# Low-rank products of a hybrid decoder: float32r parts at the start of the mixing, results kept in DRAM

## The chip, the cores and the metric

The kernel runs on one core of a Trainium2 chip. Time is in device microseconds of one execution, lower is better. Engines are named as in the profile: PE (TensorE matmul) and PEld (its weight loads), DVE (VectorE), ACT (ScalarE), POOL (GpSimd) and SP, whose queue issues nearly all DMAs.

## The reference, cut to what matters

One step of a one-layer decoder: a half-step SwiGLU FFN, a token mixing with three branches (RWKV-7, a convolution, a cross-attention into 256 memory tokens), and a second FFN. The kernel handles 512 prompt tokens and 64 sample tokens side by side, N = 576 columns, with channels on partitions. In the RWKV branch three low-rank products matter here:

```
wd, ad, gd = xm[..., c3:c4], xm[..., c4:c5], xm[..., c5:]      # 64, 64 and 160 wide
w_log = -jax.nn.softplus(-(p['w0'] + jnp.tanh(wd) @ p['w_decay_up'])) - 0.5
decay = jnp.exp(-jnp.exp(w_log))                               # = exp(-0.6065 * sigmoid(...))
a = jax.nn.sigmoid(p['a0'] + ad @ p['w_a_up'])
g = jax.nn.sigmoid(gd) @ p['w_g_up']
...
y_a = (o.reshape(b, t, D_RWKV) * g) @ p['w_rwkv_out']
```

`xm` is the token-shifted projection of the input; each product has 512 output channels, that is four blocks of 128 (one block is a pair of heads). `decay` and `a` enter the recurrence, `g` multiplies its normalised output.

## The kernel before, in words

The first FFN runs to about 430 us, the mixing from there to about 990, the merge of the branches and the second FFN after it. Large products are made of float32r parts: an operand is split into a high part, rounded to float32r by a cast on ACT (line 96), and a low part, the difference, on DVE (line 97). Three matmuls (high x high, high x low, low x high) into one PSUM bank give the product (line 110); the columns go in two halves of 288 (`H`). `proj` loads a weight block of 8 x 128 columns, splits it in pieces of 512 and makes 2 x 24 such matmuls. Small products take plain float32 operands, through `full` (line 128), which makes one matmul per operand pair and half of the columns.

The mixing starts in `lora`: `shifted(12)`, `shifted(13)` and `shifted(14)` project the low-rank inputs (win 12 holds wd and ad, 13 and 14 hold gd; 14 is only 32 wide), apply the token shift, and leave `la` (tanh on its first half) and `lg` (sigmoid). Then a list of steps, `PLAN`, runs: `A` attention, `P` `prep` of a block, `I` `inverse` and `J` `joined` of a small triangular matrix, `B` `chain` (the recurrence and the output), `G`, `C` the convolution, and `X`, `Y`, `Z`, gate projections that fill PE. In `prep` the sigmoid of `w` (tile sg, buffers u1) comes from `full("g", wda[:64], la[:64])`, then Exp, scan and reciprocal; `av` comes from `full("g", wda[64:], la[64:])`. In `chain` the gate comes last: `full("c", wg0 x lg0, wg1 x lg1)`, and DVE multiplies the result from PSUM into rs. The PSUM tags of the mixing are p (three banks, projections), g (two, prep) and c (three, chain and attention).

The order on each engine is not the order of the text: a scheduler lays the instructions of all steps on the engines by priority and by its own estimates of their durations, and each engine then runs its list strictly in order. Tiles of one name share buffers, so an instruction may also wait for a buffer's last reader. SP's list holds loads and stores alike, and a store that waits for its data holds back the loads behind it.

Of the kernel before, what the change touches and what calls it, by code (L numbers as in the profile page):

```python
# [6 lines left out]
F32 = mybir.dt.float32  # L7
F32R = mybir.dt.float32r
AF = mybir.ActivationFunctionType
ALU = mybir.AluOpType  # L10
# [40 lines left out]
class _Builder:  # L51
# [60 lines left out]
    def proj(self, src, x, n=8, m=128):  # L112

        w = self.wload(src, n * m)
        ps = []
        for h in range(2):
            p = self.bank()[:m, :H]
            self.mm3(p, w, x, n, h, m)
            ps.append((slice(h * H, (h + 1) * H), p))
        return ps  # L120
# [53 lines left out]
    def build(self):  # L174
        tc, a = self.tc, self.a
        with ExitStack() as st:
# [14 lines left out]
            self.d_g0 = [dr.tile([128, N], F32, name=f"d_g0{i}") for i in range(8)]  # L191
            self.d_ya = [dr.tile([128, N], F32, name=f"d_ya{i}") for i in range(4)]

            s_mem = ExitStack()
# [391 lines left out]
    def shifted(self, m, out, zp):  # L586

        V, A = self.V, self.A
        rows = 32 if m == 14 else 128
        p = self.proj(self.a["w14"] if m == 14 else self.a["win"][m], self.xn, 8, rows)  # L590
# [14 lines left out]
    def lora(self, lp):  # L605
        A, a = self.A, self.a
        self.ssh = lp.tile([128, 15, NB], F32, name="ssh")
        self.sho = lp.tile([128, 15, 9], F32, name="sho")
        self.wda = lp.tile([128, 512], F32, name="wda")
        self.wg = [lp.tile([128, 512], F32, name="wg0"), lp.tile([128, 512], F32, name="wg1")[:32]]  # L610
        self.G.memset(self.sho[:, 14, :], 0.0)
        self.dma(self.ssh, a["ssh"])
        self.dma(self.wda, a["wda"])
        self.dma(self.wg[0], a["wg0"])
        self.dma(self.wg[1], a["wg1"])
        self.la = lp.tile([128, N], F32, name="la")
        aux = lp.tile([128, 600], F32, name="aux")
        self.lg = [lp.tile([128, N], F32, name="lg0"), aux[:32, :N]]
        self.t11 = aux[64:96, :N].rearrange("p (h c t) -> p h c t", h=2, c=9)
        self.zz = aux[96:128, :16 * 33].rearrange("p (h c t) -> p h c t", h=2, c=8)  # L620
        self.z = [lp.tile([128, SEQ + 81], F32, name=f"z{i}") for i in range(2)]
        self.gi = lp.tile([128, PADN], F32, name="gi")
        self.st = [lp.tile([128, 128], F32, name=f"st{i}") for i in range(3)]
        self.ms = lp.tile([128, NB, 128], F32, name="ms")
        self.ax = lp.tile([128, 9, 64], F32, name="ax")
        for t in self.z:
            self.G.memset(t[:, 0:1], 0.0)
        self.G.memset(self.gi, 0.0)
        for t in self.padded(self.gi):
            self.G.memset(t[:, :, 0:1], 1.0)  # L630
        for t in self.st + [self.ms, self.ax]:
            self.G.memset(t, 0.0)
        with self.tc.tile_pool(name="lz", bufs=1, side="right") as zp:
            self.shifted(12, self.la, zp)
            A.activation(self.la[:64], self.la[:64], AF.Tanh)
            for i in range(2):
                self.shifted(13 + i, self.lg[i], zp)
                A.activation(self.lg[i], self.lg[i], AF.Sigmoid)

# [172 lines left out]
    def prep(self, j):  # L812
# [12 lines left out]
        sg = b1.tile([128, 640], F32, name="u1", bufs=2)[:, :N]  # L825
        for c, p in self.full("g", (self.wda[:64, 128 * j:128 * j + 128], self.la[:64])):
            A.activation(sg[:, c], p, AF.Sigmoid, bias=par("w0", j))
        w = b1.tile([128, PADN], F32, name="w")
# [10 lines left out]
        av = tmp("av")  # L839
        for c, p in self.full("g", (self.wda[64:, 128 * j:128 * j + 128], self.la[64:])):  # L840
            A.activation(av[:, c], p, AF.Sigmoid, bias=par("a0", j))

# [55 lines left out]
    def chain(self, j):  # L898
# [36 lines left out]
        V.tensor_tensor(rs, rs, bv, ALU.add)  # L935
        ch = slice(128 * j, 128 * j + 128)
        for c, p in self.full("c", (self.wg[0][:, ch], self.lg[0]), (self.wg[1][:, ch], self.lg[1])):
            V.tensor_tensor(rs[:, c], p, rs[:, c], ALU.mult)
        self.dbg(f"ya{j}", rs)
# [193 lines left out]
def _prep(inp):  # L1133
# [32 lines left out]
    for i in "12":  # L1166
# [4 lines left out]
    a["win"] = wt(np.concatenate([win[:, :1792], win[:, 1824:]], axis=1))  # L1171
    a["w14"] = wt(win[:, 1792:1824], 32)[0]
    a["wya"] = wt(f["w_rwkv_out"])
    a["wcb"] = wt(f["w_conv_out"])
    a["woc"] = wt(f["w_xattn_out"])
    a["wo"] = wt(f["w_o"])
    a["wda"] = np.concatenate([f["w_decay_up"], f["w_a_up"]])
    a["wg0"] = np.ascontiguousarray(f["w_g_up"][:128])
    a["wg1"] = np.ascontiguousarray(f["w_g_up"][128:])
    cols = [vec(f["ffn1_norm"]), vec(f["mix_norm"]), vec(f["ffn2_norm"]), vec(f["final_norm"]), vec(f["mu_shift"])]  # L1180
    cols += [vec(f[n].reshape(-1)) for n in ("w0", "a0", "k_k", "k_a", "r_k", "gn_g", "gn_b", "glu_b")]
# [3 lines left out]
    a["ssh"] = np.ascontiguousarray(  # L1185
        np.concatenate([f["state_shift"], np.zeros((NB, 96), f["state_shift"].dtype)], axis=1)
        .reshape(NB, 15, 128).transpose(2, 1, 0))
# [63 lines left out]
```

## Time and profile before

| what | value |
|---|---|
| median of 3 runs | 1480.89 us (1479.6 to 1481.0) |
| the profiled execution, own time | 1484.21 us |
| its span, first to last instruction | 1482.4 us |
| granted clock, mean over the span | 0.985 |
| PE busy | 1464.2 us (99%) |
| DVE, ACT busy | 1026.1 us (69%), 676.2 us (46%) |
| moved by DMA | 144.06 MB, mean 97 GB/s |

The page gives each engine's busy time, the chain of work that ended last, and groups of instructions by source line. A row of a view in order of time begins with the start in us from the span's start and a length; a row of a group has a count (x), then after the bar the busy time in us, the mean of one in ns, and the idle time before it with what ended it. A plain float32 matmul of the program stands as two records in the trace, a float32r one as one. Rows of windows give, for a stretch, the busy us of PE, PEld, DVE, ACT and POOL with counts, then the granted PE clock, the DMA share and GB/s.

### The profile page before, as it was taken

Reading aid. Unit: us, or ns where it says so; the run is one execution under the profiler, and the core shown is the slowest. Engines: PE = TensorE matmul, PEld = TensorE weight load, DVE = VectorE, ACT = ScalarE, POOL = GpSimd, SP = SyncE. Lnnn points to the kernel's source line nnn. Section 1 sums busy time; section 2 is a strip of 40 time slices with the busy share of each in tenths; the row PEclk is TensorE's granted clock in tenths of the full one; section 3 lists DMA queues with packets and bytes.
Section 4 is the critical chain, followed back from the end, with each engine's and each line's share of the span. In section 5 each row is a group of like instructions: output and inputs, shape, how many; then the busy total and the mean of one; then the engine's idle time right before and its main releaser. Section 6 shows DMA issues by size and latency. Waiting matters only on the chain.

```text
span 1482.4 us, 27100 instructions
## 1 busy us (share of the span) xinstructions
PE 1464.2 (99%) x10820; PEld 1382.3 (93%) x10820; DVE 1026.1 (69%) x2054; ACT 676.2 (46%) x1371; POOL 4.7 (0%) x22
## 2 busy tenths in 40 slices
PE   9999999999999999999999999999999999999998
PEld 9999999999998799878889878789999999999997
DVE  7976777777783569769456456357578766777775
ACT  7443434444577535445446533443354433444342
POOL 0000000000010000000000000000000000000000
PEclk9999999999999989999999999999999999999999
DMA  6222222233632244123223124345322322323221
GB/s 210 72 80 92 87 86 86 86 91 102 202 105 86 65 132 83 55 80 105 62 61 109 55 85 137 96 161 189 102 73 72 100 73 85 100 89 98 86 86 65
DMA packets 95179, 144.06 MB, mean 97 GB/s; under 512 B 43645, under 2 KB 53501, under 8 KB 95053
## 3 DMA queue, kind: packets, MB, share of 16 engines
q1 hardware_dynamic: 94476, 141.74, 31.1%
q8 instruction: 85, 1.39, 0.4%
q10 hardware_dynamic: 576, 0.59, 0.1%
q14 instruction: 42, 0.34, 0.1%
HBM read 126.07 MB, written 16.23 MB: 96 GB/s over the span
## 4 chain that ended last, share of the span: by engine, by line
PE 92%; DVE 4%; ACT 1%; DMA 1%; issue 1%; SPq 0%; DVEq 0%; POOL 0%; ACTq 0%; POOLq 0%
PE p L110 51%; PE p L382 26%; PE c L1027 1%; PE g L893 1%; PE c L1031 1%; PE c L1024 1%; DVE pr L986 1%; PE c L128 1%; PE c L1059 1%; PE g L128 1%; PE c L1057 1%; DVE cc L676 1%; PE c L1079 1%; DVE tt L988 1%; PE c L1042 1%
## 5 line engine op out<-in xcount | busy, mean ns | idle before, releaser
L110 PE MATMUL p<-x,wh 128*128 128x288 f32 x3136 | 655.6, 300 | 1.3 <-ACT kv L562 0.7
L110 PEld LDWEIGHTS p<-x,wh 128*128 128x128 f32 x3136 | 507.2, 189 | 15.2 <-issue 7.1
L110 PE MATMUL p<-x,wl 128*128 128x288 f32 x1568 | 470.0, 300 | 1.5 <-DVE wl L97 1.5
L96 ACT CAST wh<-w 128x512 fp32r<-128x512 f32 (+1 forms) x353 | 209.8, 600 | 261.9 <-PE p L382 99.8
L97 DVE TENSOR_TENSOR wl<-w,wh 128x512 fp32r<-128x512 f32 (+1 forms) x353 | 232.4, 663 | 117.4 <-ACT wh L96 110.4
L110 PEld LDWEIGHTS p<-x,wl 128*128 128x128 f32 x1568 | 295.4, 189 | 7.1 <-issue 3.1
L382 PE MATMUL p<-t,wh 128*128 128x288 f32 x1088 | 224.3, 298 | 0.0
L382 PEld LDWEIGHTS p<-t,wh 128*128 128x128 f32 x1088 | 173.8, 188 | 6.4 <-DVE t L393 6.4
L382 PE MATMUL p<-b,wh 128*128 128x288 f32 x816 | 169.7, 295 | 0.0
L382 PE MATMUL p<-t,wl 128*128 128x288 f32 x544 | 160.6, 295 | 0.0
L96 ACT CAST wh<-p 128x512 fp32r<-128x512 f32 x136 | 84.5, 621 | 156.1 <-PE p L110 117.7
L382 PEld LDWEIGHTS p<-b,wh 128*128 128x128 f32 x816 | 132.6, 188 | 0.0
L97 DVE TENSOR_TENSOR wl<-p,wh 128x512 fp32r<-128x512 f32 x136 | 93.7, 689 | 50.1 <-ACT wh L96 47.4
L382 PE MATMUL p<-b,wl 128*128 128x288 f32 x408 | 120.3, 295 | 0.0
L382 PEld LDWEIGHTS p<-t,wl 128*128 128x128 f32 x544 | 102.4, 188 | 0.0
L382 PEld LDWEIGHTS p<-b,wl 128*128 128x128 f32 x408 | 76.8, 188 | 0.0
L460 DVE SCALAR_TENSOR_TENSOR x<-p,x 128x288 f32<-128x288 f32 x128 | 57.9, 453 | 20.0 <-PE p L110 19.9
L96 ACT CAST x<-t 128x576 fp32r<-128x576 f32 (+1 forms) x60 | 36.5, 610 | 45.0 <-DVE t L464 41.8
L1051 DVE SCALAR_TENSOR_TENSOR st<-c,gc,mg 64x64 f32<-64x64 f32 x56 | 15.9, 284 | 53.3 <-PE c L1042 52.5
L372 DVE TENSOR_TENSOR p<-w 128x512 f32<-128x512 f32 x68 | 46.7, 687 | 4.2 <-DMA w<-wu 3.8
L372 DVE TENSOR_TENSOR p<-p,w 128x512 f32<-128x512 f32 x68 | 46.5, 683 | 0.2 <-DMA w<-wu 0.2
L676 DVE SCALAR_TENSOR_TENSOR cc<-up,pv,cc 128x512 f32<-128x512 f32 x60 | 43.9, 750 | 0.1
(354 smaller groups left out, 1990.8 us busy)
## 6 DMA issues: line engine op xcount, KB each, us to landing
w<-wu SPq DMA_DIRECT2D x85, 512.0 KB
w<-win SPq DMA_DIRECT2D x44, 512.0 KB
w<-wd SPq DMA_DIRECT2D x64, 256.0 KB
w<-wd SPq DMA_DIRECT2D x16, 384.0 KB
d_mb<-gate SPq DMA_DIRECT2D x16, 288.0 KB
w<-wo SPq DMA_DIRECT2D x8, 512.0 KB
d_x<-x SPq DMA_DIRECT2D x16, 144.0 KB
d_g<-gate SPq DMA_DIRECT2D x8, 288.0 KB
```

What stands on the lines that cost most here:

```text
L96: self.A.copy(hi, x)
L97: self.V.tensor_tensor(lo, x, hi.bitcast(F32), ALU.subtract)
L110: self.T.matmul(p, l, x[r][:, c], start=k == 0 and i == 0, stop=k == n - 1 and i == 2)
L128: self.T.matmul(p, l, r[:, c], start=i == 0, stop=i == len(ops) - 1)
L372: V.tensor_tensor(s, u, v, ALU.add)
L382: self.T.matmul(p, hl[l][:, c], xs[k][b][:, o], start=first and k == 0 and q == 0, stop=k == 3 and q == 2, skip_group_check=True)
L460: V.scalar_tensor_tensor(x[m][:, c], p, 0.5, x[m][:, c], ALU.mult, ALU.add)
L676: V.scalar_tensor_tensor(c[:, :SEQ], up[:, k:k + SEQ], w, c[:, :SEQ], ALU.mult, ALU.add)
L893: T.matmul(ps[:, i * 128:(i + 1) * 128], kb[o, c + i].rearrange("p a t -> p (a t)"), ra[o, c + i].rearrange("p a t -> p (a t)"), start=Tru ...
L986: V.tensor_tensor(pr, tt[:, :n, :e].unsqueeze(2).broadcast_to([np_, n, m, e]), l3[:, t:e, :e].unsqueeze(1).broadcast_to([np_, n, m, e]), A ...
L988: V.tensor_reduce(tt[:, :n, t:e], pr, op=ALU.add, axis=AX.X)
L1051: V.scalar_tensor_tensor(mn[s, s], ps[s, 256 + 64 * h:320 + 64 * h], gc[s, c:c + 1], mg[s, s], ALU.mult, ALU.add)
```

## The change

All low-rank products are made once, in a new function `low_rank`, right behind the three shifted projections at the start of the mixing. They are made of float32r parts whose low parts are stacked beside high ones: `xs` holds for wd (and for ad) the high part in 64 rows and the low part in the other 64, and the weights `wh` stand twice, so that one 128-row matmul makes high x high plus high x low, and a 64-row one (`wl`) the third term. For the gate, 128 of its 160 inputs take three matmuls, and the other 32, whose projection is now made three times over (96 weight columns), take one matmul of 96 rows. The tanh stays where it was. Sigmoids are applied to w and a as they leave PSUM; the gate is copied. All results go to DRAM: `d_w`, `d_a`, `d_gt`, four blocks each, 288 KB per block. `prep` loads `d_w` and `d_a` in place of its products, with Exp, scan and all that follows as before; `chain` loads `d_gt` and multiplies from SBUF. The tiles `wda`, `wg`, `la`, `lg` are gone from the pool lp; the pool of the new operands, lz, lies where the pool of block 0's tiles lies later, and no longer in the attention's room. Splits of a weight block cut at a multiple of its column width, which alters only the 96-wide one (pieces of 480 and 288).

```diff
     def proj(self, src, x, n=8, m=128):
-        w = self.wload(src, n * m)
+        w = self.wload(src, n * m, 512 // m * m)
...
     def shifted(self, m, out, zp):
-        rows = 32 if m == 14 else 128
+        rows = 96 if m == 14 else 128
...
-        with self.tc.tile_pool(name="lz", bufs=1, side="right") as zp:
-            self.shifted(12, self.la, zp)
-            A.activation(self.la[:64], self.la[:64], AF.Tanh)
-            for i in range(2):
-                self.shifted(13 + i, self.lg[i], zp)
-                A.activation(self.lg[i], self.lg[i], AF.Sigmoid)
+        with self.tc.tile_pool(name="lz", bufs=1) as zp:
+            self.low_rank(zp)
+
+    def low_rank(self, zp):
...
+        x = b1.tile([128, N], F32, name="k")
+        self.shifted(12, x, b1)
+        A.activation(x[:64], x[:64], AF.Tanh)
+        for i in range(2):
+            o, q = slice(64 * i, 64 * i + 64), slice(64 - 64 * i, 128 - 64 * i)
+            A.copy(xs[o, i], x[o])
+            sub(xs[q, i], x[o], xs[o, i])
+        x = b1.tile([128, N], F32, name="r")
+        self.shifted(13, x, b1)
+        A.activation(x, x, AF.Sigmoid)
+        self.split(lg[:, 0], lg[:, 1], x)
+        x = b1.tile([128, N], F32, name="av")[:96]
+        self.shifted(14, x, b1)
+        A.activation(x, x, AF.Sigmoid)
+        A.copy(gs[:96], x)
+        sub(gs[32:64], x[32:64], gs[32:64])
+
+        t = b1.tile([128, 1024], F32, name="lt")
+        self.dma(t, a["wda"])
+        t = t.rearrange("p (i c) -> p i c", i=2)
+        A.copy(wh, t)
+        for i in range(2):
+            o = slice(64 * i, 64 * i + 64)
+            sub(wl[o], t[o, i], wh[o, i])
+        t = [b1.tile([128, PADN], F32, name=n)[:, :512] for n in ("w", "g")]
+        for i in range(2):
+            self.dma(t[i], a["wg"][:, 512 * i:512 * i + 512])
+            A.copy(gh[:, i], t[i])
+        sub(gl, t[0], gh[:, 0])
+        sub(gh[64:96, 1], t[1][64:96], gh[64:96, 1])
+
+        def products(*ops):
+            for h in range(2):
+                c = slice(h * H, (h + 1) * H)
+                p = self.bank("g")[:, :H]
+                for q, (l, r) in enumerate(ops):
+                    T.matmul(p, l, r[:, c], start=q == 0, stop=q == len(ops) - 1)
+                yield c, p
+
+        for j in range(4):
+            ch = slice(128 * j, 128 * j + 128)
+            for i, (par, out, name) in enumerate((("w0", self.d_w, "bv"), ("a0", self.d_a, ("k", "r")[j % 2]))):
+                t = b1.tile([128, N], F32, name=name, bufs=2 - i)
+                o = slice(64 * i, 64 * i + 64)
+                for c, p in products((wh[:, i, ch], xs[:, i]), (wl[o, ch], xs[o, i])):
+                    A.activation(t[:, c], p, AF.Sigmoid, bias=self.par(par, j))
+                self.store(out[j], t)
+            t = b1.tile([128, N], F32, name=("av", "zt")[j % 2])
+            for c, p in products((gh[:, 0, ch], lg[:, 0]), (gh[:, 0, ch], lg[:, 1]), (gl[:, ch], lg[:, 0]),
+                                 (gh[:96, 1, ch], gs[:96])):
+                A.copy(t[:, c], p)
+            self.store(self.d_gt[j], t)
...
     def prep(self, j):
-        for c, p in self.full("g", (self.wda[:64, 128 * j:128 * j + 128], self.la[:64])):
-            A.activation(sg[:, c], p, AF.Sigmoid, bias=par("w0", j))
+        self.dma(sg, self.d_w[j])
...
-        for c, p in self.full("g", (self.wda[64:, 128 * j:128 * j + 128], self.la[64:])):
-            A.activation(av[:, c], p, AF.Sigmoid, bias=par("a0", j))
+        self.dma(av, self.d_a[j])
...
     def chain(self, j):
-        ch = slice(128 * j, 128 * j + 128)
-        for c, p in self.full("c", (self.wg[0][:, ch], self.lg[0]), (self.wg[1][:, ch], self.lg[1])):
-            V.tensor_tensor(rs[:, c], p, rs[:, c], ALU.mult)
+        gt = b3.tile([128, N], F32, name="gt")
+        self.dma(gt, self.d_gt[j])
+        V.tensor_tensor(rs, gt, rs, ALU.mult)
```

Three places show how the change moves instructions. On PE, at the end of the projection of `shifted(14)`, before:

```order
L110 MATMUL p<-x_4958,wh 32x288
L110 MATMUL p<-x_4957,wl 32x288
L110 MATMUL p<-x_4943,wh 128x288
L110 MATMUL p<-x_4944,wh 128x288
L110 MATMUL p<-x_4943,wl 128x288
```

and now (g is the PSUM tag of the products):

```order
L110 MATMUL p<-x_4970,wh 96x288
L110 MATMUL p<-x_4969,wl 96x288
L678 MATMUL g<-xs,wh 128x288
L678 MATMUL g<-xs,wl 128x288
L678 MATMUL g<-xs,wh 128x288
L678 MATMUL g<-xs,wl 128x288
L110 MATMUL p<-x_4955,wh 128x288
L110 MATMUL p<-x_4956,wh 128x288
L110 MATMUL p<-x_4955,wl 128x288
L110 MATMUL p<-x_4957,wh 128x288
L678 MATMUL g<-xs,wh 128x288
L678 MATMUL g<-xs,wl 128x288
```

Where the attention's query projections followed at once, products now stand between and among them; all but the gate products of the last block stand ahead of the first attention score (c<-kT), which follows the same number of projection matmuls as before.

On ACT, behind the token shift of `shifted(12)`: the cast of `wh` from the loaded wda (tile lt), the tanh, the casts of xs, and only then the second piece of the split of the 96-wide weights, where before a cast of 256 stood ahead of that token shift:

```order
L603 ACTIVATE zt<-z_5312,pv 128x584
L597 COPY z_5312<-ssh 96x8
L662 CAST wh<-lt 128x1024
L644 ACT_TABLE_LOAD
L644 ACTIVATE k<-k 64x576
L647 CAST xs<-k 64x576 x2
L598 COPY z_5311<-p 128x288
L599 COPY z_5311<-p 128x224
L600 COPY z_5311<-p 128x8x8
L96 CAST wh<-w 128x288
```

Further on in ACT's list the Exp of `prep` of block 0 (line 886) stands among the sigmoids (687) and gate copies (692) of the products:

```order
L692 COPY av<-g 128x288 x2
L687 ACTIVATE bv<-g,pv 128x288 x2
L687 ACTIVATE r<-g,pv 128x288
L886 ACT_TABLE_LOAD
L886 ACTIVATE w<-u_6204 128x8x64
L687 ACT_TABLE_LOAD
L687 ACTIVATE r<-g,pv 128x288
L692 COPY zt<-g 128x288
```

Its sample columns follow later with a table load before and one behind; before, the two Exp of block 0 stood behind the first softmax, and the sigmoids of a behind them.

On SP, from the load of ssh on, the loads of the weights of the products, and the stores with the first reload (u is the tile that the Exp of block 0 reads; in front of ssh two kc and two vc loads of the attention now stand, which came behind the third of the win loads before):

```order
L820 DMA kc<-ck 128x512 x2
L833 DMA vc<-cv 128x512 x2
L613 DMA ssh<-ssh 128x120
L660 DMA lt<-wda 128x1024
L668 DMA w<-wg 128x512
L668 DMA g<-wg 128x512
L86 DMA w<-win 128x1024
...
L86 DMA w<-win 128x1024 x2
L688 DMA d_w_104<-bv 128x576
L688 DMA d_a_108<-k 128x576
L881 DMA u_6204<-d_w_104 128x576
L693 DMA d_gt_112<-av 128x576
```

The reload of the first block of w stands behind the store of the first block of a; the later reloads stand some places ahead of the loads that their block needs.

More of the change, by code (lines that the diff above doesn't have):

```diff
@@ L192, in build @@
             self.d_ya = [dr.tile([128, N], F32, name=f"d_ya{i}") for i in range(4)]
+            self.d_w = [dr.tile([128, N], F32, name=f"d_w{i}") for i in range(4)]
+            self.d_a = [dr.tile([128, N], F32, name=f"d_a{i}") for i in range(4)]
+            self.d_gt = [dr.tile([128, N], F32, name=f"d_gt{i}") for i in range(4)]
             s_mem = ExitStack()
@@ L605, in lora @@
     def lora(self, lp):
-        A, a = self.A, self.a
+        a = self.a
         self.ssh = lp.tile([128, 15, NB], F32, name="ssh")
         self.sho = lp.tile([128, 15, 9], F32, name="sho")
-        self.wda = lp.tile([128, 512], F32, name="wda")
-        self.wg = [lp.tile([128, 512], F32, name="wg0"), lp.tile([128, 512], F32, name="wg1")[:32]]
         self.G.memset(self.sho[:, 14, :], 0.0)
         self.dma(self.ssh, a["ssh"])
[L613 to L616, printed above, removed]
         aux = lp.tile([128, 600], F32, name="aux")
-        self.lg = [lp.tile([128, N], F32, name="lg0"), aux[:32, :N]]
         self.t11 = aux[64:96, :N].rearrange("p (h c t) -> p h c t", h=2, c=9)
@@ L632, in lora @@
             self.G.memset(t, 0.0)
-        with self.tc.tile_pool(name="lz", bufs=1, side="right") as zp:
-            self.shifted(12, self.la, zp)
-            A.activation(self.la[:64], self.la[:64], AF.Tanh)
-            for i in range(2):
-                self.shifted(13 + i, self.lg[i], zp)
-                A.activation(self.lg[i], self.lg[i], AF.Sigmoid)
+        with self.tc.tile_pool(name="lz", bufs=1) as zp:
+            self.low_rank(zp)
+    def low_rank(self, zp):
+        V, A, T, a, b1 = self.V, self.A, self.T, self.a, self.b1
+        two = lambda name, n: zp.tile([128, 2, n], F32R, name=name)
+        sub = lambda o, x, hi: V.tensor_tensor(o, x, hi.bitcast(F32), ALU.subtract)
+        wh, wl, gh, gl = two("wh", 512), zp.tile([128, 512], F32R, name="wl"), two("gh", 512), zp.tile(
+            [128, 512], F32R, name="gl")
+        xs, lg, gs = two("xs", N), two("lg", N), zp.tile([128, N], F32R, name="gs")
+        x = b1.tile([128, N], F32, name="k")
[47 more added lines that the diff above has]
+            self.store(self.d_gt[j], t)
@@ L1171, in _prep @@
     a["win"] = wt(np.concatenate([win[:, :1792], win[:, 1824:]], axis=1))
-    a["w14"] = wt(win[:, 1792:1824], 32)[0]
+    a["w14"] = wt(np.concatenate([win[:, 1792:1824]] * 3, axis=1), 96)[0]
     a["wya"] = wt(f["w_rwkv_out"])
@@ L1176, in _prep @@
     a["wo"] = wt(f["w_o"])
[L1177 to L1180, printed above, removed]
+    a["wda"] = np.concatenate([np.concatenate([f[n]] * 2) for n in ("w_decay_up", "w_a_up")], axis=1)
+    g = f["w_g_up"]
+    a["wg"] = np.concatenate([g[:128], np.concatenate([g[128:]] * 3 + [np.zeros_like(g[128:])])], axis=1)
+    cols = [vec(f["ffn1_norm"]), vec(f["mix_norm"]), vec(f["ffn2_norm"]), vec(f["final_norm"]), vec(np.concatenate([f["mu_shift"]] + [f["mu_shift"][-32:]] * 2))]
     cols += [vec(f[n].reshape(-1)) for n in ("w0", "a0", "k_k", "k_a", "r_k", "gn_g", "gn_b", "glu_b")]
@@ L1185, in _prep @@
     a["ssh"] = np.ascontiguousarray(
-        np.concatenate([f["state_shift"], np.zeros((NB, 96), f["state_shift"].dtype)], axis=1)
+        np.concatenate([f["state_shift"]] + [f["state_shift"][:, -32:]] * 2 + [np.zeros((NB, 32), np.float32)], axis=1)
         .reshape(NB, 15, 128).transpose(2, 1, 0))
```

## The prediction

> **What bounds the kernel now.** I read the page's shares and clock row first, then the chain of waits, then who waits on PE, and only then single stretches.
>
> ```profile
> span 1482.4 us, 27100 instructions
> PE 1464.2 (99%) x10820; PEld 1382.3 (93%) x10820; DVE 1026.1 (69%) x2054; ACT 676.2 (46%) x1371; POOL 4.7 (0%) x22
> PE 92%; DVE 4%; ACT 1%; DMA 1%; issue 1%; SPq 0%; DVEq 0%; POOL 0%; ACTq 0%; POOLq 0%
> PE c L1008 <- DMA aux<-s: 2.0, 1, 2.0
> PE p L110 <- DVE wl L97: 1.5, 3, 1.1
> PE g L128 <- ACT u L827: 0.5, 2, 0.3
> ```
>
> PE is busy 99% of the span, 92% of the chain is PE, and the longest waits of PE (the last three rows, first number) are 2.0 us and less. Fillers stand between the steps of the recurrence, so a microsecond of PE work taken away anywhere is a microsecond of the span, as long as PE gets no new wait. ACT (46%) and DVE (69%) have room on average; whether they have it where the change puts its work is the question.
>
> **What is removed from PE.** The eight plain float32 products of a block of channels (two for w, two for a, four for the gate; half of the columns each) stand in the trace so, in a view of PE in order of time (start, length, instructions merged):
>
> ```profile
> 455.64 1.23 PE L128 MATMUL g<-la,wda 64*128 64x288 f32 x4
> 456.80 0.40 PE L110 MATMUL p<-x,wh 128*128 128x288 f32 x1
> 457.13 1.23 PE L128 MATMUL g<-la,wda 64*128 64x288 f32 x4
> 458.29 0.40 PE L110 MATMUL p<-x,wh 128*128 128x288 f32 x1
> 458.53 0.29 PE L110 MATMUL p<-x,wl 128*128 128x288 f32 x1
> ...
> 661.08 0.75 PE L128 MATMUL c<-lg,wg 128*128 128x288 f32 x2
> 661.76 0.75 PE L128 MATMUL c<-aux,wg 32*128 32x288 f32 x2
> 662.44 0.75 PE L128 MATMUL c<-lg,wg 128*128 128x288 f32 x2
> 663.12 0.75 PE L128 MATMUL c<-aux,wg 32*128 32x288 f32 x2
> 663.80 0.40 PE L110 MATMUL p<-x,wl 128*128 128x288 f32 x1
> 664.04 0.43 PE L110 MATMUL p<-x,wh 128*128 128x288 f32 x2
> 664.31 0.29 PE L110 MATMUL p<-x,wl 128*128 128x288 f32 x1
> 664.43 0.43 PE L110 MATMUL p<-x,wh 128*128 128x288 f32 x2
> 664.70 0.29 PE L110 MATMUL p<-x,wl 128*128 128x288 f32 x1
> ```
>
> Lengths overlap, so starts must be subtracted. From wl at 664.31 to wl at 664.70 are three float32r matmuls: 0.39/3 = 0.13 us each. A plain float32 product is two records. The w and a products of block 0 take 458.53 - 455.64 = 2.89, less two float32r matmuls that stand among them, 2.89 - 0.26 = 2.63 us; the gate products 664.04 - 661.08 = 2.96, less one, 2.83 us. Four blocks: 4 x (2.63 + 2.83) = 21.8 us. With the 0.5 us that PE waited at L128 for ACT, 22.3 us go.
>
> **What is added to PE.** Per block and half of the columns 2 + 2 + 4 float32r matmuls, 64 in all. At 0.13 that is 8.3 us, the lower end. The trace has no 64-row float32r part. What a change of operand height costs I take from float32: two equal products in a row take 456.80 - 455.64 = 1.16, 0.58 each; alternating 128 and 32 rows, 661.76 - 661.08 = 0.68 each, 0.10 more. The 16 wl parts are 64 rows high between 128-row ones: 32 changes, 3.2 us. If the 96-row gate part counts too, 16 more, 1.6 us. Ends 8.3 and 13.1; I take 11.5, the 64-row parts being like the case seen and the 96-row part possibly not. A gain from overlap with the 128-row part before it is excluded: both use the same rows. The last low-rank projection grows from 32 to 96 weight columns:
>
> ```profile
> 435.98 0.29 PE L110 MATMUL p<-x,wl 128*32 128x288 f32 x1
> 436.37 0.29 PE L110 MATMUL p<-x,wl 128*32 128x288 f32 x1
> 442.24 0.29 PE L110 MATMUL p<-x,wl 128*128 128x288 f32 x1
> 442.63 0.29 PE L110 MATMUL p<-x,wl 128*128 128x288 f32 x1
> ```
>
> Three matmuls take 0.39 with 32 columns and with 128, so this is 0. PE thus loses 22.3 - 11.5 = 10.8 us of work (ends 9.2 and 14.0).
>
> **What it costs at the opening.** All products, sigmoids, evacuations and splits now come in one stretch, on ACT. Busy time by window (span, then PE, PEld, DVE, ACT) and ACT's rows in 430 to 470:
>
> ```profile
> 430.00:442.00 12.00, 12.00 (x94) 10.91 (x93) 11.52 (x48) 8.77 (x20) 1.13 (x2) 1.00 0.71 203
> 442.00:455.60 13.60, 13.60 (x100) 12.88 (x98) 3.71 (x6) 6.64 (x17) 0.53 (x1) 1.00 0.48 156
> L96 ACT CAST wh<-w 128x512 fp32r<-128x512 f32 x9 | 5.6, 620 | 8.7 <-PE p L110 6.2 <-DMA w<-win 2.4
> L723 ACT COPY q<-p 128x288 f32<-128x288 f32 x4 | 1.6, 389 | 1.8 <-PE p L110 1.8
> L841 ACT ACT_TABLE_LOAD x1 | 1.3, 1283 | 0.0
> L841 ACT ACTIVATE av<-g,pv 128x288 f32<-128x288 f32 x2 | 1.0, 504 | 0.0
> L832 ACT ACTIVATE w<-u 128x512 f32<-128x512 f32 (+1 forms) x2 | 0.9, 443 | 0.0
> ```
>
> Up to the first attention score (c<-kT, 454.7 before) the changed program has on ACT, beyond the 8.77 + 6.64 = 15.4 us of these windows: 16 sigmoids at 0.50 = 8.0; 8 gate copies at 0.39 = 3.1; casts of wh (two 512s), gh (two), xs (two), lg, gs at 0.62 = 5.0; 0.4 for the second piece of the w14 split; four more table loads at 1.28 = 5.1, because prep 0's two Exp stand among the sigmoids; those Exp, 0.9. That is 22.5, together 37.9 us. PE has 25.6 + 11.5 = 37.1 us there. So ACT turns from 60% busy into the bound of this stretch: at least 0.8 us of PE stall. Behind it wait PE (two g banks, and weight parts) and DVE (wl after wh).
>
> Two loads can make it more. ACT's cast of wh now stands ahead of the second piece of the w14 split and waits for wda, on SP's queue behind two kc and two vc loads. And prep 0's Exp (w<-u) waits for a store of d_w and its reload, behind a d_a store.
>
> ```profile
> 430.97 0.84 SPq L86 DMA_DIRECT2D w<-win  x2
> 435.11 1.29 ACT L96 CAST wh<-w 128x512 fp32r<-128x512 f32 x2 [1.19 <-DMA w<-win]
> ```
>
> The nearest price of a transfer: 512 KB issued at 430.97 let ACT go at 435.11, 4.1 us. If wda lands a whole such transfer late, 4.1 us. Store and reload of 288 KB, at most 8.2 us, against some 7 us that ACT has between storing sigmoid and Exp (two gate copies, six sigmoids, two casts, a q copy and a table load: 0.8 + 3.0 + 1.2 + 0.4 + 1.3), leave 1 to 2 us, and 2 more if the d_a store holds the queue. The ends are 0.8 and 0.8 + 4.1 + 3.5 = 8.4; I take 3.5, nearer the lower end, because both loads have most of their time covered.
>
> **What costs nothing.** The later loads of u, av and gt are 12 of 288 KB, with 12 stores 7 MB on 144; all but the first stand far ahead of their use on SP, and the filler projections cover them. Uncovered, one costs 4.1 us of ACT or DVE, not of PE. In the chain tail DVE now multiplies from SBUF instead of PSUM, with PE on fillers. DVE gains some eight subtractions at the opening, where its 11.52 of 12.00 are convolution taps that can stand behind. The table loads of the whole program stay 43.
>
> **Sum.** -22.3 + 11.5 + 3.5 = -7.3 us. The span of 1482.4 goes to 1475.1, the profiled execution's own 1484.2 to 1476.9. The median of the runs, 1480.9, lies 3.3 under that execution, so the median forecast is 1473.6.
>
> **A rule against the sum.** The granted clock falls at times, and PE's stalls could bring more of it:
>
> ```profile
> 870.70:877.60 6.90, 6.90 (x55) 5.70 (x53) 4.67 (x14) 3.35 (x10) 0.00 (x0) 1.00 0.03 6
> 877.60:884.40 6.80, 6.80 (x25) 4.29 (x25) 2.13 (x4) 0.70 (x3) 0.00 (x0) 0.50 0.23 80
> ```
>
> The clock (third number from the right) is 0.50 for 6.8 us here, which loses 3.4 us. The Trainium skill, page "TensorE: Matmul & The Clock Gate", section "Why this matters for your kernels", says to leave no idle gap over some 3 us between bursts. By it stalls of this size, in pieces, cost nothing further. The trace does not quite agree: PE was busy 6.90 of 6.90 us before that drop, with thin matmuls. Joining of block 0 now stands right beside prep 1's thin products, so one drop more or less, 3.4 us either way, goes into the range.
>
> **The rivals.**
> - ACT keeps up. The loads come in time, the 64-row parts cost no change: -22.3 + 8.3 + 0.8 = -13.2, 1467.7; with 11.5, 1470.9. For it: DVE and ACT have few waits on DMA before. Against: the 37.9 on 37.1 us.
> - The opening eats the gain. Both upper ends: -22.3 + 13.1 + 8.4 = -0.8, 1480.1, no change. For it: ACT runs strictly in order there.
> - Slower: the round trip of d_w in the middle of the products. The Exp of block 0 waits, ACT behind it frees no g bank and splits no weights, and PE stops. It decides once PE's stall exceeds 10.8 us. If the transfers take twice 4.1 each because win and kc loads of 256 and 512 KB stand ahead, ACT waits 16.4 + 2 - 7 = 11.4 us and PE falls into one half-clock stretch, 3.4 more: with 0.8, -10.8 + 15.6 = +4.8, 1485.7. Against: the first attention loads are issued earlier now and may be through by then.
> - The parts don't stream at 0.13: if each took half of a plain float32 product, 0.58/2 = 0.29, 64 x 0.29 = 18.6 and the changes 3.2: -22.3 + 21.8 + 3.5 = +3.0, 1483.9, about no change.
>
> **How the numbers follow.** About 0.2% (3 us) can be told from no change. Forecast (1470.9 to 1477) 0.52; ACT keeps up 0.19; opening eats the gain 0.16; slower 0.09; parts too slow 0.04. Faster takes the first two and a little of the third, 0.74; no change the rest of the third and most of the last, 0.17; slower 0.09. The forecast itself spans 1470 to 1477. The range of 8 in 10 reaches from 1466, short of a full gain with a clock drop less, to 1481, where the opening eats the gain.
>
> **What will show it.** Right: products on PE between the w14 projection and the first attention score, 8 to 13 us of PE busy in place of 21; ACT close to full from the end of the w14 projection to that score, which comes some 14 us later than 454.7; PE idle there of 2 to 6 us, released by ACT (g banks, wh) or DVE (wl); the same 43 table loads. Wrong: PE idle over 10 us there with ACT waiting on DMA for u or lt; g<-xs matmuls much over 0.2 us from start to start; or a different number of half-clock stretches later that moves the time by itself.

## The result and the profile after

| | before | after |
|---|---|---|
| median of the runs | 1480.95 us (1479.6 to 1481.1) | 1501.63 us (1494.4 to 1505.0) |
| ratio to before | | 1.0130 (1.0099 to 1.0161) |
| profiled execution: own time, span | 1484.21, 1482.4 us | 1502.43, 1500.6 us |
| mean granted clock of it | 0.985 | 0.974 |

The kernel is slower by 20.7 us; a later set of runs on another chip gave 1502.4 us and 1.0139 (1.0111 to 1.0167). From the page of after, the span, the busy times, the clock row and the chain by engine; the last row is the clock row of before:

```profile
span 1500.6 us, 27176 instructions
PE 1475.4 (98%) x10820; PEld 1395.3 (93%) x10820; DVE 1027.8 (68%) x2059; ACT 681.9 (45%) x1387; POOL 4.6 (0%) x22
PEclk9999999999999999999798998999999999999999
PE 89%; DVE 6%; ACT 2%; DMA 1%; issue 1%; SPq 0%; DVEq 0%; POOL 0%; ACTq 0%; POOLq 0%
PEclk9999999999999989999999999999999999999999
```

PE is still the bound, but DVE now has 6% of the chain (4% before), and the clock row shows a 7 and two 8s among its slices between 700 and 950 us (before has a single 8). The longest waits of PE in after (us in total, times, longest), and as the last row the one of before at the place of the first:

```profile
PE g L138 <- ACT u L908: 5.2, 3, 2.1
PE p L110 <- DVE wl L97: 4.5, 5, 1.9
PE c L1069 <- ACT aux L1064: 1.5, 2, 0.9
PE g L138 <- ACT u L855: 1.2, 2, 0.7
```

The first are the sums over a head of k's squares in `prep`, which wait for the square on ACT. Outside 440 to 1010 us the two traces agree within 1 us.

**Where 18.2 us of span came from.** I gave each stretch between the starts of two successive PE matmuls to the tile of the first, less the part in which PE was idle and less half of the part in which the clock stood at 0.50:

| us of PE | before | after | difference |
|---|---|---|---|
| plain products g<-la,wda; c<-lg,wg; c<-aux,wg | 19.6 | 0 | -19.6 |
| parts: g<-xs,wl 5.2; g<-xs,wh 4.1; three gate groups 4.7 | 0 | 14.0 | +14.0 |
| all other matmuls | 1423.9 | 1425.2 | +1.3 |
| PE idle | 10.8 | 17.4 | +6.6 |
| lost to the half clock | 20.5 | 35.8 | +15.3 |

(The sum is 17.7; 0.5 us more lie behind PE's last matmul.) The work fell, by 4.3 us. What rose is idle time and, more than twice as much, the half clock. Its longest stretch stands in block 2. The view by windows (span, PE, PEld, DVE, ACT, POOL busy, then clock, DMA share, GB/s) of after:

```profile
729.70:733.10 3.40, 3.40 (x55) 3.08 (x51) 2.17 (x4) 1.83 (x5) 0.00 (x0) 1.00 0.03 9
733.10:750.20 17.10, 17.10 (x71) 13.70 (x71) 8.29 (x11) 5.91 (x13) 0.00 (x0) 0.50 0.09 18
750.20:760.00 9.80, 9.80 (x70) 7.57 (x69) 3.68 (x9) 3.00 (x11) 0.00 (x0) 1.00 0.43 129
```

and of before, at the same place of the program:

```profile
717.20:720.60 3.40, 3.17 (x52) 2.94 (x51) 1.88 (x3) 0.58 (x1) 0.00 (x0) 1.00 0.02 6
720.60:727.40 6.80, 6.80 (x32) 5.54 (x31) 1.23 (x4) 2.67 (x6) 0.00 (x0) 0.50 0.14 24
727.40:737.00 9.60, 9.60 (x73) 8.01 (x73) 2.88 (x7) 5.06 (x12) 0.00 (x0) 1.00 0.11 31
```

PE is busy throughout, but for 0.23 us ahead of the drop in before. The clock falls to one half behind a run of small matmuls in both, and stayed there 17.1 us in place of 6.8. PE in order of time at that place, after:

```profile
727.59 1.16 PE L946 MATMUL g<-ra,kb 64*128 64x128 f32 x8
728.67 1.20 PE L1061 MATMUL c<-aux,gr 32*32 32x32 f32 x32
729.79 1.16 PE L946 MATMUL g<-ra,kb 64*128 64x128 f32 x8
730.88 1.19 PE L1069 MATMUL c<-gr,aux 32*32 32x32 f32 x32
732.00 1.16 PE L946 MATMUL g<-ra,kb 64*128 64x128 f32 x8
...
740.60 0.59 PE L110 MATMUL p<-x,wh 128*128 128x288 f32 x1
```

Rows are left out at the dots. For 13.0 us (7.5 of them at half clock) no projection stands among the small matmuls, and those ahead of the drop use half (64 rows) or a sixteenth (32 rows, 32 columns) of the array. The same run took 11.2 us before (714.84 to 726.08, 5.5 of them at half clock). What follows differs: in before projections come one after another, and full clock is back at 727.4; in after small products (c<-vu,gr and c<-xs,gr) stand between them until 746.1, and full clock comes back at 750.2.

**A measure of thin use.** In all traces the half-clock stretches of the mixing last 3.4, 6.8, 10.2, 13.7, 17.1 or 20.5 us, multiples of 3.4. So for windows of 3.4 us I added up what each matmul uses: rows/128 x columns/128 x time. As a scale of my own I counted 0.12 us for 288 columns in float32r (a little less than the 0.13 from start to start in the traces), and twice that for each of the two records of plain float32. By this scale the densest projections give 0.91. In the windows ahead of the 20 drops (starts of half-clock stretches) in the two profiles, the use was between 0.01 and about 0.4; some other windows of 0.33 to 0.42 had no drop, and runs of one kernel differ in which ones drop. So I call "thin time" of a kernel the total of all moments, from 480 us to the end of the mixing and with half-clock stretches shrunk to their length at full clock, from which the next 3.4 us stay under 0.36. It is 30.3 us before and 42.3 us after.

**Time and clock.** In 67 runs of the kernel before (1474.9 to 1490.8 us) the time is 1462.6 us + 1349 us x (1 - clock), with a correlation of 0.97. So time x clock tells what a run would have taken without the losses: 1460.7 us before (median), 1466.1 after; the rest, 22 and 37 us, is clock. Of the 20.7 us, about 5.4 are work and waits and about 15 are clock; in the table above, of one profile each, they are 2.3 and 15.3.

### The profile page after: what moved, and what is told of

Its sections match the earlier page's. It is cut to its first block, busy times and chain, and to the rows that moved or that the text cites. A ratio compares the mean times of both kernels' runs of the same rounds, so it can differ in the third digit from the quotient of the medians.

```text
span 1500.6 us, 27176 instructions
## 1 busy us (share of the span) xinstructions
PE 1475.4 (98%) x10820; PEld 1395.3 (93%) x10820; DVE 1027.8 (68%) x2059; ACT 681.9 (45%) x1387; POOL 4.6 (0%) x22
## 4 chain that ended last, share of the span: by engine, by line
PE 89%; DVE 6%; ACT 2%; DMA 1%; issue 1%; SPq 0%; DVEq 0%; POOL 0%; ACTq 0%; POOLq 0%
PE p L110 49%; PE p L385 25%; PE g L946 1%; PE c L1080 1%; DVE pr L1039 1%; DVE wl L97 1%; PE c L1077 1%; PE c L1084 1%; PE g L678 1%; PE c L1112 1%; DVE tt L1041 1%; PE c L1110 1%; PE g L138 1%; PE c L1132 1%; DVE cc L731 1%
## 5 line engine op out<-in xcount | busy, mean ns | idle before, releaser
L110 PE MATMUL p<-x,wh 128*128 128x288 f32 x3136 | 665.6, 304 | 1.9 <-ACT kv L565 0.7
L110 PEld LDWEIGHTS p<-x,wh 128*128 128x128 f32 x3136 | 514.5, 191 | 13.9 <-issue 5.2
L110 PEld LDWEIGHTS p<-x,wl 128*128 128x128 f32 x1568 | 299.2, 191 | 10.3 <-DVE wl L97 6.4
```

What stands on the lines that cost most here:

```text
L110: self.T.matmul(p, l, x[r][:, c], start=k == 0 and i == 0, stop=k == n - 1 and i == 2)
```

## The experiments

All medians, with intervals of the ratio to runs of the kernel before on the same chip (1481.3 to 1482.7 us). The last three columns: the median of time x clock, what the clock took, and the thin time of the profile. (At full clock, x1_pool leaves out one run whose clock reads 0.935 at 1483.5 us, off the line of the others.)

| kernel | us | ratio (interval) | at full clock | lost | thin |
|---|---|---|---|---|---|
| before, all runs | 1482.2 | | 1460.7 | 22 | 30.3 |
| after, first and second set | 1501.6, 1502.4 | 1.0130, 1.0139 | 1466.1, 1467.0 | 37, 35 | 42.3, 43.5 |
| x1_pool | 1481.1 | 0.9995 (0.9974 to 1.0017) | 1460.7 | 21 | 30.5 |
| x2_gate_early | 1478.4 | 0.9971 (0.9952 to 0.9990) | 1459.2 | 19 | 32.6 |
| x3_wa_early | 1486.1 | 1.0027 (1.0008 to 1.0045) | 1465.3 | 21 | 36.6 |
| x4_dense | 1510.2 | 1.0182 (1.0151 to 1.0213) | 1483.4 | 27 | 40.5 |
| x5_warm | 1494.9 | 1.0093 (1.0073 to 1.0114) | 1469.7 | 25 | 38.5 |
| x7_full_rows | 1492.6 | 1.0082 (1.0057 to 1.0106) | 1463.2 | 30 | 44.7 |
| x8_gate_early_wa_place | 1490.9 | 1.0065 (1.0045 to 1.0086) | 1461.4 | 29 | 34.1 |
| x9_free | 1476.1 | 0.9968 (0.9939 to 0.9997) | 1454.6 | 21 | 36.0 |
| x11_gr_fill | 1508.0 | 1.0161 (1.0126 to 1.0197) | 1479.2 | 29 | 40.8 |
| x13_r_first | 1483.7 | 1.0011 (0.9995 to 1.0026) | 1459.5 | 25 | 35.4 |
| x14_after_r_first | 1488.5 | 1.0049 (1.0022 to 1.0076) | 1463.5 | 25 | 35.3 |
| x15_before_r_first | 1492.2 | 1.0071 (1.0039 to 1.0104) | 1464.9 | 28 | 39.4 |
| x16_weights_first | 1490.9 | 1.0076 (1.0044 to 1.0109) | 1460.8 | 28 | 38.2 |

**The parts of the change.** My first theory was cover: the dense products stood among thin work, and without them PE idles and its clock falls. The rivals: the scheduler's new order, or the opening. First a control, before with one edit:

```diff
-        with self.tc.tile_pool(name="lz", bufs=1, side="right") as zp:
+        with self.tc.tile_pool(name="lz", bufs=1) as zp:
```

> The kernel before, with one edit: the pool of the shifted projections' tiles lies at the left, as in the change, so that the early attention loads may come ahead; no product is touched. Theory C (cover): what is lost comes from the dense products taken out of prep and chain, so that PE idles or works thinly there and its clock halves more often; nothing is taken out here, so 1478 to 1484 us, mean clock 0.983 to 0.987. Rival R (order): the loss is the new order that the scheduler finds once rooms and loads move, whatever is taken out; then this kernel has a good part of it, 1488 to 1500 us and a clock below 0.981.

1481.1 us: moving the pool costs nothing. Then half of the change each (excerpts, against the changed kernel):

```diff
 x2_gate_early: prep as before
-        self.dma(sg, self.d_w[j])
+        for c, p in self.full("g", (self.wda[:64, ...], self.la[:64])):
 x3_wa_early: chain as before
-        self.dma(gt, self.d_gt[j])
+        for c, p in self.full("c", (self.wg[0][:, ch], self.lg[0]), (self.wg[1][:, ch], self.lg[1])):
```

> Of the change only the gate: its products early as float32r parts, through DRAM, gone from chain; w and a as before in prep. Work alone, by the changed kernel's trace: 10.8 us less at the old places, 4.7 us of products and about 1 us for the 96 wide projection more, so -5 us. Theory C: chain loses its cover, prep keeps it: half-clock time between the 41 us of before and the 72 of the change, 1478 to 1490 us, and no new idle time of PE ahead of prep's sums (it was 1.3 to 2.1 us each in three blocks). Rival O (opening): the loss is made where the products now stand; then no new half-clock stretches behind 500 us and 1476 us. Rival R: as slow as the whole change, 1495 us or more, with the same places slow.

> Of the change only w and a: early, float32r, through DRAM; the gate as before in chain. Work alone: 8.8 us less in prep, 9.3 us more at the opening, so +0.5 us. Theory C: prep loses its cover, so PE idles ahead of prep's sums as in the change (1.3 to 2.1 us each in two or three blocks) and the clock halves behind: 1485 to 1497 us, clock 0.976 to 0.983; with the gate-only kernel's difference it adds up to about the +20 us of the whole change. Rival O: +0.5 us and no new idle time in prep, 1479 to 1483 us. Rival R: the two parts do not add up: one of them has all of it, or each has all of it.

The gate alone is a small gain, 1478.4, the only version here that is faster than both kernels and computes the reference; w and a alone cost 3.9 us. Together they should have given the time of before, not 20 us more. The waits at the sums that x3_wa_early was to bring did not come:

```profile
PE p L110 <- ACT gate L838: 4.1, 2, 2.6
PE g L138 <- ACT u L894: 1.1, 1, 1.1
```

They are 1.1 us there (0.4 in x2_gate_early), no more than before, and the clock is 0.986. At full clock the halves nearly add up (-1.5 and +4.6, whole +5.4 to +6.3); the clock does not: neither half loses more than before, the whole 13 to 15 us more. Was the whole a bad draw?

> The changed kernel once more, timed in as many rounds as the gate-only (1478.4 us) and the w-and-a-only kernel (1486.1 us), whose differences from before (-3.9 and +3.9 us) do not add up to the +20 us of the first four runs of the whole. If the first runs were typical: 1494 to 1505 us, a mean clock of 0.974 to 0.982. If they were a bad draw of the moments at which the clock is judged: a median of 1480 to 1490 us at 0.984 or more.

1502.4 us at 0.974 to 0.980: no.

**Work put back.** If cover was missing, useless dense work should pay for itself in part.

```diff
 x4_dense, beside the loads of sg and av, and of gt
+        self.dense("g", slice(0, 64)) ... self.dense("g", slice(64, 128)) ... self.dense("c", slice(0, 128), slice(0, 32))
 x5_warm, behind self.shifted(4 + j, k, b1)
+        for i in range(3 * (j > 0)):
+            p = self.bank("g")[:, :H]
+            for q in range(6):
+                T.matmul(p, self.xn[i][0][:, :128], self.xn[q][0][:, :H], start=q == 0, stop=q == 5)
 x11_gr_fill, behind each multiply into gr
+                d = self.bank("g")[:, :H]
+                for q in range(3):
+                    T.matmul(d, self.xn[h][0][:, :128], self.xn[q][0][:, :H], start=q == 0, stop=q == 2)
```

> The changed kernel, with 32 plain float32 matmuls of the old sizes put back in prep and chain, on constants, and read by nobody: 19.6 us of PE work by the trace of before. Theory C: they cover again what the removal laid bare; the idle time ahead of prep's sums goes and half-clock time falls from 72 us to 40 to 55, so the time rises by much less than the work, 1498 to 1508 us, clock above 0.980. Rivals R and O: 19.6 us of work on a full engine are 19.6 us, 1518 to 1524 us, with the same half-clock stretches.

> The changed kernel, with 18 dense float32r matmuls (128 rows, 288 columns, results read by nobody) in prep of blocks 1 to 3 behind the projection of k, where PE now idles 1.3 to 2.1 us ahead of prep's sums: 54 x 0.13 = 7 us of PE work more. Theory C' (the thin stretches): they fill the idle time (5.2 us of waits at the sums) and raise the use of the array there, so that the half-clock stretches that follow these three places go, 10 us of half clock, 5 us of loss: 2 to 6 us faster than the changed kernel on the same chip. Rival (the clock falls elsewhere or by chance): the idle time is filled, the clock is as before, 0.977, and the time within 2 us of the changed kernel's or above it.

> The changed kernel, with three dense float32r matmuls (128 rows, 288 columns, read by nobody) behind each of the six groups of small 64-row products (tile gr) of each prep: 72 x 0.13 = 9.5 us of PE work, some 2 to 5 us more for the changes of height. Of all its thin stretches the longest is there, 13.3 us of small matmuls in block 2, and the half-clock stretch behind it lasted 17.1, 10.2 and 20.5 us in three profiles (6.8 us before). Theory C: with their use raised, that stretch and the ones in the other blocks shrink: half-clock loss 36 to 20 to 27 us, clock 0.982 to 0.986, the time within 4 us of the changed kernel's 1502 us in spite of 12 us of work. Rival (the clock falls by chance or for other reasons): 1511 to 1517 us, clock 0.975 to 0.979.

x4_dense added 19.3 us of matmuls and 8 to 9 us of time: it took back 8 to 10 us of clock, less than hoped. x5_warm gained most: 7.4 us more work and 7.5 us less time, with 10 us less lost to the clock. Not as I had said, though: of the waits at the sums (5.1 us in the second profile of the changed kernel) 3.7 us stayed. In blocks 1 and 2 the fillers ended some 4 us ahead of the sums, and the half clock behind them stayed; only block 3's wait and its half-clock stretch (6.8 and 10.2 us in the two profiles of the changed kernel) went. The long stretch of block 2 (17.1 and 10.2 us) went too, and no filler stands there. x11_gr_fill missed: 12.6 us of fillers and 2.5 us more on the small products among them, 5.6 to 6.4 us more time, and the long half-clock stretch still 13.7 us. All three lose less to the clock, 25 to 29 us against 35 to 37. But each edit also gives the scheduler a new order, and these runs do not separate the two, so it is not shown that the fillers did it.

**The price of the 64-row parts.** Two products (of w or of a, two matmuls each) in order of time, after; four matmuls in 1.30 us:

```profile
450.45 0.40 PE L678 MATMUL g<-xs,wh 128*128 128x288 f32 x1
450.78 0.40 PE L678 MATMUL g<-xs,wl 64*128 64x288 f32 x1
451.10 0.40 PE L678 MATMUL g<-xs,wh 128*128 128x288 f32 x1
451.43 0.39 PE L678 MATMUL g<-xs,wl 64*128 64x288 f32 x1
451.75 0.54 PE L110 MATMUL p<-x,wh 128*128 128x288 f32 x2
```

```diff
 x7_full_rows
-            sub(wl[o], t[o, i], wh[o, i])
+        sub(wl, t, wh)
-                for c, p in products((wh[:, i, ch], xs[:, i]), (wl[o, ch], xs[o, i])):
+                for c, p in products((wh[:, i, ch], xs[:, i]), (wl[:, i, ch], xs[:, i])):
```

> The changed kernel, with the third term of w and a in 128 rows (the low part of the weights stands twice, as the high part does) in place of 64: 16 matmuls of 64 rows become ones of 128. In the trace such a 64-row part stretched PE by about 0.39 us beyond its matmuls. If that is the price of the change of height, products of w and a fall from 9.3 to 32 x 0.13 = 4.2 us, and the time by 4 to 6 us against the changed kernel on the same chip. Rival (the pitch is due to the weights or to PSUM): within 1 us of it.

The same products with 128 rows throughout, four in 0.54 us:

```profile
445.56 0.29 PE L676 MATMUL g<-xs,wh 128*128 128x288 f32 x1
445.69 0.30 PE L676 MATMUL g<-xs,wl 128*128 128x288 f32 x1
445.83 0.30 PE L676 MATMUL g<-xs,wh 128*128 128x288 f32 x1
445.96 0.29 PE L676 MATMUL g<-xs,wl 128*128 128x288 f32 x1
446.10 0.43 PE L110 MATMUL p<-x,wh 128*128 128x288 f32 x2
```

So a matmul of 64 rows between ones of 128 costs (1.30 - 0.54)/2 = 0.38 us beyond its own 0.13, and more rows with more arithmetic are cheaper. w and a fell from 9.3 to 4.9 us. The time fell by 9.8 us, more than that; some 5 us came from the clock, which this run does not explain.

**Half the work in place.** Gate early, w and a as 128-row parts in `prep`:

> The gate-only kernel (gate early, through DRAM), and w and a in prep as before, but as float32r parts of 128 rows kept in SBUF (the low weights of w and of a share one tile, so that each third term also has low weights of the other on its low inputs, as small as the low x low term that is left out anyway); the loaded gate takes the room of kbt, which is done by then. Work: gate -5 us as in the gate-only kernel, w and a 8.8 us to 4.2 us, so -10 us against before. If prep and chain keep cover enough: 1468 to 1474 us. If half the products in prep are too little cover, PE idles ahead of prep's sums as in the changed kernel (1 to 2 us in three blocks) and the clock falls: 1478 to 1488 us.

1490.9 us, above both expectations. By the account of PE's time above, its work is 12.9 us less than before, but its idle time 13.8 us more (24.6 us); one wait for a DMA (aux, in the joining of a block) grew from 2.0 to 6.5 us. The clock took 29 us with a thin time of only 34.1; the measure does not explain this one.

**The removal by itself.** Without the parts of three blocks (48 of the 64 product matmuls, not 48 x 2 as the expectation has it), nearly all of the removed work is simply gone; w, a and the gate of these blocks are then not the reference's.

```diff
 x9_free, in products
+                if j:
+                    yield c, lg[:, 0].bitcast(F32)[:, c]
+                    continue
```

> The changed kernel with the matmuls of the low-rank products of blocks 1 to 3 left out at the opening (48 x 2 halves fewer parts; the sigmoids and copies read a tile in SBUF instead, stores and reloads stay): three quarters of the 14.0 us that the products cost PE there, 10.5 us, are gone, so that 19.6 us of PE work were taken out of prep and chain and only 3.5 us and the wider projection put in. Theory C (the dense products were cover): the idle time and the half-clock time behind 500 us stay as in the changed kernel, so 1502 - 10.5 - 0 to 4 for half-clock drops at the opening: 1487 to 1492 us, slower than before although some 14 us of work are gone. Rival O (the opening is what made it slow, and what follows is noise): the loss goes with it, 1465 to 1474 us, clock 0.985 or more.

1476.1 us at a clock of 0.9855, 2 us above what the rival of the opening expected at most and 11 us under the least that the theory of cover expected: cover falls in this form. The same products were taken out of `prep` and `chain` as in the changed kernel, PE idles as much (19.1 us), and yet the clock is that of before. Windows of 500 to 1000 us, before, after and then this kernel (clock third from the right):

```profile
500.00:1000.00 500.00, 491.41 (x3611) 426.64 (x3610) 308.67 (x682) 228.59 (x521) 0.00 (x0) 0.96 0.32 93
```

```profile
500.00:1000.00 500.00, 486.15 (x3519) 425.19 (x3519) 302.54 (x678) 218.35 (x515) 0.00 (x0) 0.93 0.30 88
```

```profile
500.00:1000.00 500.00, 488.42 (x3686) 431.50 (x3685) 323.27 (x718) 226.57 (x525) 0.00 (x0) 0.97 0.35 102
```

What differs, beside the opening, is the order: with other work at the opening the scheduler lays the whole mixing anew, and its thin time is 36.0 us in place of 42.3. That an order moves the clock with the opening kept is what x14_after_r_first shows below.

**The order alone.** In `prep`, r's projection written ahead of the sums that PE waits at; not a matmul added or taken. In the full-rows kernel (x13), in the changed one (x14) and in before (x15):

```diff
         self.shifted(4 + j, k, b1)
+        self.shifted(j, r, b1)
         sq = b1.tile([128, 640], F32, name="u1", bufs=2)[:, :N]
...
-        self.shifted(j, r, b1)
         for o, x, y in zip(ra_r, parts(r), after):
```

> The kernel with the full rows (1492.6 us), and in prep the projection and token shift of r written ahead of the sums of k's squares instead of behind them; no PE work is added or taken. There PE waits 5.2 us for the square of k in blocks 1 to 3. Theory C: another projection stands ahead of the sums, so the 5.2 us of waits shrink to under 2 and the half-clock stretches behind them (two or three) go too: 1480 to 1487 us, clock 0.983 or more. Rival (the wait goes to the next step of prep, which is as long; or the scheduler had placed that projection there already): 1490 to 1496 us.

> The changed kernel itself, with r's projection and token shift written ahead of the sums of k's squares in prep; no work is added or taken. Theory D (order): the half clock is set by how long the scheduler's order leaves the array thinly used (by the PE rows of each trace, starts from which the next 3.4 us use under 0.36 of it: 30 us before, 43 us in the changed kernel, 35 and 36 us in the two kernels with the same removal and a clock of 0.983 and more); then this order brings it to 33 to 38 us, the loss from 36 to 20 to 28 us and the time from 1502 to 1486 to 1494 us. Rival C (the removal itself): 1498 us or more, clock under 0.979.

> The kernel before with the same step alone: r's projection written ahead of the sums. Its waits at the sums are 1.2 us and its thin time 30 us. Theory D with the changed kernel's order as an unlucky one: nothing much to gain here, 1477 to 1486 us, thin time 28 to 36 us. Rival (the step is an improvement by itself, of any such kernel, by 9 us as in the full-rows kernel): 1470 to 1475 us.

The same edit makes the full-rows kernel 8.9 and the changed kernel 13 to 14 us faster, and before 10 us slower, outside both of its expectations. In the changed kernel the wait at the sums fell from 5.2 us in three blocks to this (waits of PE, x14_after_r_first):

```profile
PE g L148 <- ACT u L155: 1.2, 1, 1.2
PE g L138 <- ACT u L909: 1.0, 1, 1.0
```

while PE's whole idle time stayed at 17.4 us, so the gain is mostly clock, from 36 to 25 us, with the thin time going from 42.3 to 35.3. In before the thin time went the other way, 30.3 to 39.4 us, the clock's loss from 22 to 28 us; 4 us more are work and waits. The thin time was worked out from the profile after each run; it explains, it did not forecast. The step is no improvement by itself: what it changes is the draw. Last, the weights of the products loaded and cast ahead of the first shifted projection, on top of x13:

> The kernel with full rows and r first (1483.7 us, 2.0 us of PE waiting ahead of the 96-row projection for a cast on ACT), and the loads, casts and differences of the products' weights written ahead of the first shifted projection. If only that wait goes: 1480 to 1483 us. Theory D: the scheduler also lays the rest anew, by which the time can move either way by 5 us or so: 1476 to 1489 us, and the low-use time of its trace tells which way (35 us now: less than 33 goes with under 1481 us, more than 38 with over 1486 us).

1490.9 us, above the 1489 expected at most. The wait for the cast on ACT went and another took its place: 2.2 us ahead of the first product, for the difference of xs on DVE. The thin time rose from 35.4 to 38.2 us, which by the expectation goes with over 1486 us; one wait of PE for a DMA (aux) took 5.7 us, much as in x8. In x8 the loaded gate lies in the room of kbt; here it does not, so such a wait does not need that.

Over all kernels and their lost time, thin time has a correlation of 0.77; x7 (44.7 us, 30 lost) and x8 (34.1, 29 lost) stand off the line. It is a property of one profile, and what keeps the clock down once it is down is not in it.

## Why the prediction was wrong, point by point

I forecast 1473.6 us, faster; it was 1501.6.

- **"More or less one drop, 3.4 us either way, into the range"**: this step failed. Half-clock time between 500 and 1000 us went from 41.0 us in 7 stretches to 71.7 us in 13, a loss of 15.3 us more. I took the order of the mixing behind the opening as given, but for the one neighbourhood that I named. The scheduler laid all of it anew; x14_after_r_first and x15_before_r_first show that such an order moves either kernel by 10 us or more at the same work. The prediction's last sign of being wrong was just this, another number of half-clock stretches later, but the sum gave it no price beyond one drop.
- **"A microsecond taken away anywhere is a microsecond of the span, as long as PE gets no new wait."** The condition did not hold. PE's idle time grew by 6.6 us, 4.0 of it at the sums. How this looks, in the view of all engines in order of time (after, prep of block 1, other rows left out):

```profile
592.01 0.23 ACT L600 COPY z<-p 128x64 f32<-128x64 f32 x1
592.39 0.78 ACT L603 ACTIVATE zt<-z,pv 128x584 f32<-128x584 f32 x1
592.97 0.29 PE L110 MATMUL p<-x,wh 128*128 128x288 f32 x1
593.20 0.75 DVE L605 SCALAR_TENSOR_TENSOR k<-z,omu,zt 128x512 f32<-128x512 f32 x1
593.87 0.28 DVE L606 SCALAR_TENSOR_TENSOR k<-z,omu,zt 128x64 f32<-128x64 f32 x1
594.19 0.78 ACT L908 ACTIVATE u<-k,pv 128x576 f32<-128x576 f32 x1 [0.78 <-DVE k L606]
595.01 0.61 PE L138 MATMUL g<-cst,u 128*128 128x2 f32 x4 [1.75 <-ACT u L908]
```

  The token shift goes from ACT to DVE and back to ACT, 3 us, and PE reaches the sums before it is through. I had listed the waits that went (0.5 us at L128) and asked nothing about those that PE would reach earlier. Whether the removal itself brings this wait is not shown. In x3_wa_early and x2_gate_early PE's idle time rises too, by 3.9 and 3.5 us, but at other places, with 1.1 and 0.4 us at the sums; and in x15_before_r_first, where nothing is removed, it rises by 2.2. What is shown is that little of the saved work reached the span: in x7, x13, x16 and x8 PE's work, counted as above, is 7 to 13 us less than before, and its idle time 9 to 14 us more.
- **What is removed, -21.8 us**: 19.6 measured. I scaled from the products quoted, of one block; over all blocks they were cheaper, 2.2 us for w and a and 2.7 for the gate.
- **What is added, +11.5 us**: 14.0. The 0.13 us of a part was right, and that 96 rows cost no change too. The changes of height were mis-sized: I took 3.2 us for all. The parts of w and a alone took 9.3 us in place of 32 x 0.13 = 4.2, so 5.1 more; with 128 rows throughout (x7_full_rows) they take 4.9.
- **The opening, +3.5 us of stall**: 0.6 us in the profile; 2.3 us in the second one, for a cast on ACT, with a half-clock stretch of 3.4 us behind it. From 430 us to the first score ACT was busy for 33.2 of 39.3 us, where 37.9 had been counted, so it did not become the bound. The windows, before and after:

```profile
430.00:500.00 70.00, 69.41 (x476) 60.46 (x475) 42.05 (x112) 49.60 (x127) 1.66 (x3) 1.00 0.31 96
```

```profile
430.00:500.00 70.00, 69.36 (x446) 59.50 (x445) 40.09 (x105) 56.96 (x134) 0.47 (x1) 1.00 0.44 141
```

  Fourth busy time: ACT, 49.60 to 56.96 us of 70. PE, the first, is unmoved. The first attention score came at 469.28 us against 454.69, 14.6 us later, where some 14 had been forecast (and 11.5 + 3.5 = 15.0 is in the sum): that came out by luck, as more work and less stall met.
- **The later loads, the round trip of d_w, DVE: nothing.** Right: no wait of PE, ACT or DVE names d_w, d_a or d_gt. So the forecast's slower rival, the Exp that waits for its reload, did not occur; slower came by a way that none of the rivals described. The rival of slow parts fell with the 0.13.
- **The page's rule** (the Trainium skill, "TensorE: Matmul & The Clock Gate", "Why this matters for your kernels": keep gaps under some 3 us). I noted that the trace did not quite agree and priced it as one drop. The traces part from it further: no gap ahead of a drop in after is over 2.2 us, and 6 of its 13 drops have none at all in the 3.4 us ahead of them, only thin matmuls.

## What to carry to other kernels

Where PE is the bound and its clock drops in some windows, read time x clock and the clock's loss apart, before and after an edit: here some 5 us were work and waits and some 15 the clock. That an order can move the clock's loss by this much is shown; whether the removal raises it on average is not. Kernels with the whole removal lost 21 to 37 us to it, three orders of before (before, x1_pool, x15) 21 to 28. Ask of dense work that is taken out not only what it costs, but which waits and which runs of small matmuls it stood among. And where a scheduler lays the order anew at each edit, one timing is one draw: a second order of the same work (here one line moved) showed 13 to 14 us, and 10 us in the other direction for before, so a small edit is judged over several orders.

## What the runs showed of the hardware that was not expected

- The half clock can come with PE 100% busy: it came after 3.4 us whose use of the array is about 0.4 or less (0.91 for dense projections), though not after all such windows. In one place it stayed for 17.1 us in which PE did not wait at all; 3.4 us of nearly nothing but projections ended it.
- A kernel with 7.4 us of useless dense matmuls more was 7.5 us faster (x5_warm); how much of this is the filling and how much the new order is open.
- A float32r matmul of 64 rows between ones of 128 cost 0.38 us beyond its 0.13; one of 96 rows nothing (two in 0.27 us from 449.66 in the changed kernel).
- Single runs of one kernel spread over 16 us (1474.9 to 1490.8), and their time follows the granted clock with a correlation of 0.97.

Open remain why just the changed kernel's order came out thin, since nothing in the edit asks for it; what in the order holds the clock down beyond the thin time (x7, x8); and why the clock falls at some thin windows and not at others, which the 3.4 us steps suggest but do not prove.
